# Early sub-keys of a two-layer transformer's PEER stage: weights split ahead by way of DRAM, products in three passes, and one-hot rows of eight tokens

## The chip, the cores and the metric

The kernel runs on one core of a Trainium2 chip. The metric is the device time of one execution in microseconds (us); it is measured in several runs, and their median is given. One further execution is recorded by the hardware profiler, and all the rows below are from it. The engines are named PE (TensorE, matmuls), PEld (TensorE's weight loads, which overlap PE), DVE (VectorE), ACT (ScalarE), POOL (GpSimd) and SP (SyncE, which issues most DMAs). All arithmetic is in float32 or in split products that stand for it.

## What is computed

Two layers over 512 latent tokens and 256 context tokens of width 1024. The lines of the reference that matter:

```python
u  = h * (1 + mod[:, 1]) + mod[:, 0]                  # modulate
pl = split_pieces(u @ w_mix)                          # one projection for four mixers
y  = merge_branches(u, (oa, ob, oc, od), w_gate, w_branch[l], w_out[l])
#    m = sum(sigmoid(u @ w_gate_i) * (o_i @ w_branch_i));  y = m @ w_out
h  = layer_norm(DEEPNORM_ALPHA * h + mod[:, 2] * y, ln_attn[l])
u2 = h * (1 + mod[:, 4]) + mod[:, 3]
y2 = peer_ffn(u2, peer_wq[l], peer_subkeys[l], peer_u[l], peer_v[l])
h  = layer_norm(DEEPNORM_ALPHA * h + mod[:, 5] * y2, ln_ffn[l])

def peer block(xb):                                   # 128 tokens
    s = einsum('thpk,hpnk->thpn', q, subkeys)         # 8 heads, 2 halves, 128 sub-keys
    sv, si = top_k(s, 16)
    fv, fi = top_k(all 16 x 16 sums of sv, 16)        # 16 of 16384 experts for each head
    e = first sub-key * 128 + second sub-key;  gate = softmax(fv)
    act = gelu(einsum('thkd,td->thk', tab_u[e], xb))
    return einsum('thk,thkd->td', gate * act, tab_v[e])
```

Layer 0 computes context and latent tokens; layer 1 needs only latent tokens after the mixers.

## The kernel before

**PEER, dense and sparse.** Tokens come in blocks of 128: six in layer 0, four in layer 1. For most of them (four in layer 0, three in layer 1, so `nt` is 512 or 384 columns) the expert stage is dense: for each first sub-key `j` of 128, all 128 experts are computed as a 128 x `nt` product of the table's slice `peer_ut[l, j]` (1024 x 128 floats, 512 KB) with the modulated tokens, Gelu, times a matrix `G` of gates, times `peer_v`. The other blocks gather their experts' rows by indirect DMA on POOL, beside the dense stage.

**Split products.** A float32 product that has to be exact enough is made of three matmuls of type fp32r: `split` (L107 to L110) rounds a value to its high part by an ACT copy and takes the low part by a DVE subtraction, and `mm3` (L113 to L118) multiplies high by high, high by low and low by high into the same PSUM bank. The dense stage does that for `act` (weights `du`) and `acc`, and so do the projections, the branch gates (`gate_sigmoid`, `gate_product`, weights `gw` from `wgb`) and the queries (`wq`). Products whose operands are plain float32 are issued as two matmul records each.

**The stages of a layer**, in order of the program: modulation, projections (`project_all`), `mix`, output projection, `peer_front` (layer norm, queries, the top 16 of each half), the gate stage, the dense stage, the finish. In the profiled run layer 0's mixers stand from some 240 to 560 us, its gate stage from some 1081 to 1366, and layer 1's from 2870 to 3315 and from 3484 to 3708.

**`mix`** runs the four branches in the order d, b, a, c as a generator. After each step it pays in pieces of filler: gate sigmoids (`sg`, whose result `gs` goes to DRAM as `sig`) and gate products (`pr`), by a rate for each branch (`PACE`). In layer 1 the steps also advance `mod_columns`, which makes two columns of modulation from weights that come in 512 KB loads (`wmodc`, two buffers) and are multiplied by DVE at L326. Raw q and k of each head group come back from DRAM as `src`, with `SRC` = 3 buffers.

**The gate stage** makes `G`. `chosen` (L1383 on) finds the 16 experts of each token and head, with index searches (L1404 and L1408) and predicated copies that fetch the sub-keys' numbers (L1447 to L1451), and transposes sub-keys and gates into `sT` (`pst`). `build_gates` takes `GT` = 4 tokens at a time: DVE compares a row of numbers with the tokens' sub-keys (L1474), which gives one-hot rows `ohA` and `ohB` of 4 x 128 elements, in `OHB` = 5 buffers each; ACT scales each token's `ohB` by its gates (L1480); PE multiplies the two for each token (L1484); ACT copies the product into `gs`, from where it goes to DRAM. In the third and fourth block `BD` = 1 and 2 of four tokens are compared and scaled by DVE in one instruction (L1482) in place of the long comparison and ACT.

**Early sub-keys.** So that PE has work in the gate stage, the first products of `EARLY` = 21 sub-keys in layer 0 and 26 in layer 1 are made there (`early_pieces`). For each, one 512 KB load fetches `eu` (two buffers), eight matmuls of 512 or 384 columns multiply it with `u2`, a plain float32 copy of the modulated tokens that `modulate` keeps, ACT does the Gelu, and the result goes to DRAM as `ge`. `UP` gives the share of these pieces that is due before the first one-hot row (33% and 48%), and the rest is spread over the steps of `build_gates`; in layer 0 pieces of the next layer's modulation stand among them. The dense stage then loads `ge` for these sub-keys instead of computing it.

**What sets the order.** The program is written in the Tile framework, whose scheduler places each instruction on its engine's queue by priority and readiness in a modelled time line; `tc.later(n)` lowers the priority of what stands in it, `issue_after` binds it behind an instruction. Each engine then works through its queue in order, so an instruction that waits holds all behind it. SP's queue of DMA issues is one of these.

## Time and profile before

| | us |
|---|---|
| median of 3 runs | 4694.86 |
| lowest and highest | 4692.51, 4699.5 |
| the profiled execution | 4695.4 |
| its span in the profile | 4693.6 |
| PE busy in the span | 4506.4 |
| DVE busy | 3708.0 |
| ACT busy | 2310.1 |
| POOL busy | 1004.5 |

The mean clock granted to TensorE over the span was 0.982 of full speed. The busy times are sums over the whole program, which goes through stages with different limits. For a stage one reads the stretch of time that it takes: how long each engine is busy in it, and what its waits end on. A busy PE is modelled from pipelined matmuls, so it isn't PE at its peak.

### The profile page before, as it was taken

The numbers are of one execution on the slowest core, as the hardware profiler recorded it, in microseconds if no ns is written. First come the engines' busy times: TensorE is split into PE (matmuls) and PEld (weight loads), VectorE is DVE, ScalarE is ACT, GpSimd is POOL, SyncE is SP. The second block draws the span as 40 slices with busy tenths as digits, with TensorE's granted clock in tenths as the row PEclk, the third lists the DMA queues.
The fourth block names the chain that finished last, engine by engine and source line by source line (L and its number), as shares of the span: only waits on it lengthen the run. The fifth ranks groups of instructions, "written<-read, shape, count | busy, mean of one in ns | idle before, by whom it ended". The sixth has DMA issues, their size and how long they took to land.

```text
span 4693.6 us, 67460 instructions
## 1 busy us (share of the span) xinstructions
PE 4506.4 (96%) x24113; PEld 3820.5 (81%) x24113; DVE 3708.0 (79%) x7649; ACT 2310.1 (49%) x4214; POOL 1004.5 (21%) x772
## 2 busy tenths in 40 slices
PE   8999999999999999999999798898999999999998
PEld 6978888885668888888888697787877788888887
DVE  7857555899979889898889975866698777777777
ACT  4357554325964444344334454665328744444444
POOL 0000000000005545555555200000000043333431
PEclk9999999999999999999999899999999999999999
DMA  7844332523679999999999676542426798888885
GB/s 276 293 144 125 105 99 90 206 78 115 182 246 339 347 337 348 341 346 348 343 341 345 215 280 189 176 145 87 168 89 179 246 351 309 303 310 295 313 304 196
DMA packets 495793, 1120.39 MB, mean 239 GB/s; under 512 B 43312, under 2 KB 244832, under 8 KB 486368
## 3 DMA queue, kind: packets, MB, share of 16 engines
q1 hardware_dynamic: 384864, 713.38, 44.9%
q0 software_dynamic: 110592, 402.70, 23.9%
q8 instruction: 190, 3.11, 0.3%
q14 instruction: 147, 1.20, 0.1%
HBM read 975.14 MB, written 140.80 MB: 238 GB/s over the span
## 4 chain that ended last, share of the span: by engine, by line
PE 73%; issue 8%; DVE 7%; ACT 5%; DMA 4%; POOL 2%; SPq 0%; POOLq 0%; DVEq 0%; ACTq 0%
PE act L115 5%; PE act L117 5%; PE act L116 5%; PE acc L117 5%; PE acc L115 5%; PE acc L116 5%; PE S L1506 4%; PE mm L117 3%; PE mm L115 3%; PE mm L116 3%; PE mm L1484 3%; PE sg L115 3%; PE sg L116 3%; PE sg L117 3%; PE mm L124 2%
## 5 line engine op out<-in xcount | busy, mean ns | idle before, releaser
L1678 POOL DMA_INDIRECT gu<-peer_u,pe x384 | 494.7, 1288 | 3049.5 <-DMA du<-peer_ut 2515.8
L1690 POOL DMA_INDIRECT gu<-peer_v,pe x384 | 509.6, 1327 | 569.4 <-PE acc L117 252.4
L115 PE MATMUL act<-u2T,duh 128*128 128x512 f32 (+1 forms) x1656 | 603.5, 364 | 11.8 <-ACT duh L109 11.8
L117 PE MATMUL act<-u2T,dul 128*128 128x512 f32 (+1 forms) x1656 | 603.4, 364 | 0.7 <-DVE dul L110 0.7
L116 PE MATMUL act<-u2T,duh 128*128 128x512 f32 (+1 forms) x1656 | 602.8, 364 | 0.0
L115 PE MATMUL acc<-dvh,dwh 128*128 128x512 f32 x1536 | 598.5, 390 | 2.3 <-ACT dwh L109 2.3
L116 PE MATMUL acc<-dvl,dwh 128*128 128x512 f32 x1536 | 599.4, 390 | 0.0
L1696 DVE SCALAR_TENSOR_TENSOR gy<-gu,gwt,gy 128x1024 f32<-128x1024 f32 x381 | 488.2, 1281 | 106.1 <-DMA gu<-peer_v,pe 102.5
L117 PE MATMUL acc<-dvh,dwl 128*128 128x512 f32 x1536 | 546.6, 391 | 1.8 <-DVE dwl L110 1.8
L1681 DVE SCALAR_TENSOR_TENSOR gu<-gu,px 128x1024 f32<-128x1024 f32 x384 | 462.6, 1221 | 92.7 <-DMA gu<-peer_u,pe 91.9
L109 ACT ACTIVATE dwh<-dw 128x512 fp32r<-128x512 f32 (+1 forms) x256 | 147.8, 578 | 555.9 <-DVE dw L1566 553.0
L1565 ACT ACTIVATE dw<-Gt 128x512 f32<-128x512 f32 (+1 forms) x256 | 260.3, 1020 | 278.3 <-DVE dwl L110 274.7
L109 ACT ACTIVATE dvh<-dv 128x1024 fp32r<-128x1024 f32 x256 | 263.4, 1052 | 206.9 <-PE rot L117 122.8
L115 PEld LDWEIGHTS act<-u2T,duh 128*128 128x128 f32 x1656 | 312.2, 189 | 50.3 <-ACT duh L109 12.5
L110 DVE TENSOR_TENSOR dvl<-dv,dvh 128x1024 fp32r<-128x1024 f32 x256 | 309.5, 1220 | 52.6 <-ACT dvh L109 52.5
L116 PEld LDWEIGHTS act<-u2T,duh 128*128 128x128 f32 x1656 | 312.3, 189 | 37.3
L117 PEld LDWEIGHTS act<-u2T,dul 128*128 128x128 f32 x1656 | 312.1, 188 | 37.2 <-DVE dul L110 2.3
L117 PEld LDWEIGHTS acc<-dvh,dwl 128*128 128x128 f32 x1536 | 287.8, 188 | 65.7 <-DVE dwl L110 6.2
L115 PEld LDWEIGHTS acc<-dvh,dwh 128*128 128x128 f32 x1536 | 288.3, 188 | 60.8 <-ACT dwh L109 4.0
L116 PEld LDWEIGHTS acc<-dvl,dwh 128*128 128x128 f32 x1536 | 288.3, 188 | 57.5
L1484 PEld LDWEIGHTS mm<-ohB,ohA 128*128 128x128 f32 x1792 | 234.0, 193 | 98.8 <-ACT ohB L1480 48.7
L1506 PE MATMUL S<-u,eu 128*128 128x384 f32 (+1 forms) x752 | 310.7, 537 | 2.0 <-ACT ege L1509 1.2
(396 smaller groups left out, 10873.8 us busy)
## 6 DMA issues: line engine op xcount, KB each, us to landing
dv<-peer_v SPq DMA_DIRECT2D x256, 512.0 KB, 6.1
du<-peer_ut SPq DMA_DIRECT2D x207, 512.0 KB, 6.3
G<-gsb SPq DMA_DIRECT2D x26, 2048.0 KB, 9.3
wmodc<-wmodc SPq DMA_DIRECT2D x84, 512.0 KB, 5.1
gw<-wgb SPq DMA_DIRECT2D x128, 256.0 KB, 2.9
Gt<-G SPq DMA_DIRECT2D x31, 1024.0 KB, 8.3
eu<-peer_ut SPq DMA_DIRECT2D x49, 512.0 KB, 3.8
Gt<-G SPq DMA_DIRECT2D x31, 768.0 KB, 6.7
```

Of the source, the lines that this page charges most:

```text
L109: a = self.nc.scalar.activation(hi, src, AF.Copy)
L110: return a, self.nc.vector.tensor_tensor(lo, src, hi, op=OP.subtract)
L115: mm(out, lh, rh, start=first, stop=False)
L116: mm(out, lh, rl, start=False, stop=False)
L117: self.pe = mm(out, ll, rh, start=False, stop=last)
L1484: self.last = nc.tensor.matmul(ps[:, s % 4, :], A[:, s, :], B[:, s, :], start=True, stop=True)
L1506: nc.tensor.matmul(ps[:, :n], U[:, k, :], uf[:, k, :], start=k == 0, stop=k == KC - 1)
L1565: nc.scalar.activation(W, self.Gt[:, :, j % JB], AF.Copy)
L1678: dma = nc.gpsimd.indirect_dma_start(out=t, out_offset=None, in_=I['peer_u'], in_offset=bass.IndirectOffsetOnAxis(ap=e[:, k:k + 1], axis=0))
L1681: nc.vector.scalar_tensor_tensor(t, t, 1.0, x, op0=OP.mult, op1=OP.mult, accum_out=act[:, k:k + 1])
L1690: dma = nc.gpsimd.indirect_dma_start(out=t, out_offset=None, in_=I['peer_v'], in_offset=bass.IndirectOffsetOnAxis(ap=e[:, k:k + 1], axis=0))
L1696: nc.vector.scalar_tensor_tensor(y, t, w[:, k:k + 1], y, op0=OP.mult, op1=OP.add)
```

## The change

1. **Weights split ahead.** A new generator, `split_early`, runs in `mix`. It takes the slices `peer_ut[l, j]` of the early sub-keys in parts: halves of 128 x 512 in layer 0 (42 parts), quarters of 128 x 256 in layer 1 (104). Each part is loaded into `eur` (`PREB` = 2 buffers), split by an ACT copy into `eus` (one buffer) and a DVE subtraction in place, and both halves are stored in a DRAM tile `eu`. `mix` advances it by `PRE` parts for each step of a branch: 3 in layer 0's branch d, 2 in layer 1's branches d, a and c. In layer 0 what is left is done, and its pool given back, before the sum `m` is allotted at the end of branch d; in layer 1 it shares the mixers' pool, and what is left is done at the end of `mix`.
2. **Products in three passes.** `early_pieces` loads the two halves (`euh`, `eul`, 512 KB each, two buffers each) from `eu` and calls `mm3` with the split tokens `uT` that the dense stage uses. The plain copy `u2` is gone, and `modulate` loses its argument `keep`. `first_u` has a tile of its own.
3. **Eight tokens at a time.** `GT` goes from 4 to 8, `OHB` from 5 to 3, and `BD` from 1 and 2 of four tokens to 2 and 4 of eight. L1474 (L1487 after) compares 8 x 128 elements in one instruction.
4. **`SRC`** is 3 in layer 0 and 2 in layer 1.

The diff, cut to its core:

```diff
-PKB, BIG, VB, SRC, GK = (8, 4, 4, 3, 4)
-GT, OHB = (4, 5)
+PKB, BIG, VB, SRC, GK = (8, 4, 4, (3, 2), 4)
+GT, OHB = (8, 3)
-BD = (0, 0, 1, 2)
+BD = (0, 0, 2, 4)
+PREB = 2
+PRE = ({'d': 3}, {'d': 2, 'a': 2, 'c': 2})
+PREK = (4, 2)
...
-            u = keep[:, k, c0:c0 + n] if keep is not None else pool.tile([128, 512], F, name="uf", bufs=3 if tok else 2)[:, :n]
+            u = pool.tile([128, 512], F, name="uf", bufs=3 if tok else 2)[:, :n]
...
+            self.eu = self.dram.tile([EARLY[l], 2, 128, KC, 128], F, name=f"eu{l}")
...
-                fill = [self.early_pieces(l, i, uf, tp) for i in range(EARLY[l])]
+                fill = [self.early_pieces(l, i, uT, nd * 128, tp) for i in range(EARLY[l])]
...
+            ep = tc.alloc_tile_pool(name="eus", bufs=2, side="right", reuse_waits="tile") if self.need else self.ap
...
+            pre = self.split_early(l, ep)
             at = 0
             for kind, done in self.branches(l, blocks, order):
                 at += 1
+                for _ in range(PRE[l].get(kind, 0)):
+                    next(pre, None)
...
                     if kind == 'd':
+                        if self.need:
+                            for _ in pre:
+                                pass
+                            ep.release()
                         self.dp.release()
...
+    def split_early(self, l, p):
+        nc, w = self.nc, PREK[l]
+        parts = [(i, j, slice(h, h + w)) for i, j in enumerate(early(l)) for h in range(0, KC, w)]
+        raw = []
+        for n, (i, _, ks) in enumerate(parts):
+            while len(raw) < min(n + PREB, len(parts)):
+                U = p.tile([128, w, 128], F, name="eur", bufs=PREB)
+                nc.sync.dma_start(U, self.I['peer_ut'][l, parts[len(raw)][1]][:, parts[len(raw)][2]])
+                raw.append(U)
+            hi = p.tile([128, w, 128], R, name="eus", bufs=1)
+            self.split(hi, raw[n][:].bitcast(R), raw[n])
+            for x, u in enumerate((hi[:].bitcast(F), raw[n])):
+                nc.sync.dma_start(self.eu[i, x][:, ks], u)
+            yield
...
-            U = p.tile([128, KC, 128], F, name="eu", bufs=2)
-            nc.sync.dma_start(U, self.I['peer_ut'][l, j])
+            U = [p.tile([128, KC, 128], R, name="eu" + x, bufs=2) for x in "hl"]
+            for x, u in enumerate(U):
+                nc.sync.dma_start(u[:].bitcast(F), self.eu[i, x])
             return U
...
-                nc.tensor.matmul(ps[:, :n], U[:, k, :], uf[:, k, :], start=k == 0, stop=k == KC - 1)
+                self.mm3(ps[:, :n], (U[0][:, k, :], U[1][:, k, :]), (uT[0][:, k, :n], uT[1][:, k, :n]), k == 0, k == KC - 1)
```

**Where the instructions stand.** PE, layer 0's gate stage, at its first one-hot products. `mm<-ohB,ohA` are the products of one-hot rows, one for each token; `S<-u_10140,eu` is an early product of 512 columns. Before:

```order
L1506 MATMUL S<-u_10140,eu 128x512
L1484 MATMUL mm<-ohB,ohA 128x128 x4
L1506 MATMUL S<-u_10140,eu 128x512
L1484 MATMUL mm<-ohB,ohA 128x128 x4
L1506 MATMUL S<-u_10140,eu 128x512
L1484 MATMUL mm<-ohB,ohA 128x128 x4
```

The same place now; `u2T_10432` and `u2T_10433` are the high and the low parts of the tokens, `euh` and `eul` those of the weights:

```order
L1497 MATMUL mm<-ohB,ohA 128x128 x8
L119 MATMUL S<-u2T_10432,euh 128x512
L120 MATMUL S<-u2T_10433,euh 128x512
L121 MATMUL S<-u2T_10432,eul 128x512
L119 MATMUL S<-u2T_10432,euh 128x512
L120 MATMUL S<-u2T_10433,euh 128x512
L121 MATMUL S<-u2T_10432,eul 128x512
L1497 MATMUL mm<-ohB,ohA 128x128 x8
```

One early product stood behind each four one-hot products; now one or two, of three passes each, stand behind each eight.

DVE, layer 0's gate stage, from the last instructions ahead of the first one-hot rows. `fi` and `fv` are the index searches of `chosen`, `t` and `tm` its predicated copies, `c` a copy of the candidates, `c_iota` the row of numbers. Before:

```order
L1408 MAX_INDEX fi<-fv,c_13468 128x8
L1407 MAX fv<-c_13474 128x8
L1449 COPY_PREDICATED t_12891<-tm,t_12891 128x64
L1474 TENSOR_TENSOR ohA<-c_iota,pst_10138 128x512
L1474 TENSOR_TENSOR ohB<-c_iota,pst_10138 128x512
L1474 TENSOR_TENSOR ohA<-c_iota,pst_10138 128x512
L1474 TENSOR_TENSOR ohB<-c_iota,pst_10138 128x512
```

Now:

```order
L1460 COPY_PREDICATED t_13333<-tm,sif 128x512
L1487 TENSOR_TENSOR ohA<-c_iota,pst_10437 128x1024
L1487 TENSOR_TENSOR ohB<-c_iota,pst_10437 128x1024
L1487 TENSOR_TENSOR ohA<-c_iota,pst_10437 128x1024
L1487 TENSOR_TENSOR ohB<-c_iota,pst_10437 128x1024
L1487 TENSOR_TENSOR ohA<-c_iota,pst_10437 128x1024
L1487 TENSOR_TENSOR ohB<-c_iota,pst_10437 128x1024
L1445 TENSOR_TENSOR a_13311<-fi,t_13315 128x128
L1462 COPY_PREDICATED t_13321<-tm,t_13321 128x64x4
L1419 MATCH_REPLACE c_13914<-fv,cand 128x112
L1421 MAX_INDEX fi<-fv,c_13908 128x8
L1462 COPY_PREDICATED t_13333<-tm,t_13333 128x64x4
```

The first rows stood behind the last searches and copies of the next blocks; now rows of twice the length stand ahead of a part of these.

ACT, layer 1's mixers, in branch c. `PTh`, `oT` and `OT` are copies out of PSUM for which PE waits, `P` the exponentials. Before:

```order
L882 ACTIVATE PTh<-mm 128x4x128
L882 ACTIVATE PTh<-mm 128x128
L855 ACTIVATE oT_31560<-mm 128x512
L896 ACTIVATE OT<-mm 128x256
L1004 ACTIVATE P,sums<-S,nms 128x512
L882 ACTIVATE PTh<-mm 128x4x128
L109 ACTIVATE gwh<-gw 128x256
L859 ACTIVATE oT_31561<-mm 128x512
```

Now:

```order
L895 ACTIVATE PTh<-mm 128x4x128
L895 ACTIVATE PTh<-mm 128x128
L113 ACTIVATE eus<-eur 128x256
L868 ACTIVATE oT_31546<-mm 128x512
L113 ACTIVATE eus<-eur 128x256
L909 ACTIVATE OT<-mm 128x256
L1017 ACTIVATE P,sums<-S,nms 128x512
L895 ACTIVATE PTh<-mm 128x4x128
L872 ACTIVATE oT_31547<-mm 128x512
L895 ACTIVATE PTh<-mm 128x128
L1017 ACTIVATE P,sums<-S,nms 128x640
L113 ACTIVATE eus<-eur 128x256
```

The splits of the weights (`eus<-eur`) stand between these copies, each behind its own load.

## Rows read from the trace of the kernel before

**Rows 1.** Page, part 1: busy us (share of the span) and instructions.
```profile
PE 4506.4 (96%) x24113; PEld 3820.5 (81%) x24113; DVE 3708.0 (79%) x7649; ACT 2310.1 (49%) x4214; POOL 1004.5 (21%) x772
```

**Rows 2.** Windows: us, then busy us (instructions) per engine, clock, DMA share, GB/s.
```profile
165.00:240.00 75.00, 75.00 (x627) 74.98 (x627) 65.72 (x130) 25.71 (x46) 0.00 (x0) 1.00 0.76 253
240.00:400.00 160.00, 146.38 (x824) 121.90 (x823) 96.95 (x220) 98.82 (x208) 0.00 (x0) 0.96 0.45 136
2870.00:3080.00 210.00, 190.12 (x906) 148.98 (x907) 150.61 (x311) 134.46 (x274) 0.00 (x0) 0.95 0.53 161
3080.00:3315.00 235.00, 220.41 (x1256) 185.99 (x1255) 151.71 (x297) 136.79 (x295) 0.00 (x0) 0.99 0.37 114
1081.00:1130.00 49.00, 44.19 (x106) 19.35 (x105) 49.00 (x302) 14.97 (x24) 0.00 (x0) 0.99 0.47 156
1130.00:1262.00 132.00, 122.28 (x660) 88.09 (x661) 127.62 (x398) 127.88 (x361) 0.00 (x0) 0.97 0.56 164
1262.00:1366.00 104.00, 103.57 (x601) 74.26 (x601) 90.44 (x241) 83.86 (x219) 0.00 (x0) 1.00 0.67 193
3484.00:3536.00 52.00, 50.77 (x160) 29.84 (x159) 51.72 (x297) 16.80 (x33) 0.00 (x0) 1.00 0.44 134
3545.00:3650.00 105.00, 102.14 (x612) 81.06 (x611) 83.08 (x168) 102.96 (x304) 0.00 (x0) 1.00 0.67 199
```

The engines stand in the order PE, PEld, DVE, ACT, POOL.

**Rows 3.** Time line of PE, early products: start us, us, instruction, records.
```profile
1080.92 32.78 PE L1506 MATMUL S<-u,eu 128*128 128x512 f32 x76
...
3483.40 36.29 PE L1506 MATMUL S<-u,eu 128*128 128x384 f32 x112
...
3702.46 5.33 PE L1506 MATMUL S<-u,eu 128*128 128x384 f32 x16
```

**Rows 4.** Windows, as in rows 2: 200 us of layer 0's dense stage.
```profile
1400.00:1600.00 200.00, 200.00 (x884) 165.59 (x883) 180.03 (x297) 83.26 (x98) 103.55 (x80) 1.00 0.92 341
```

**Rows 5.** Groups of DVE instructions, whole span: busy us, mean ns, idle before.
```profile
L1404 DVE FIND_INDEX8 fi<-fv,cand 128x8 uint32<-128x112 f32 x80 | 20.3, 266 | 0.0
...
L1449 DVE COPY_PREDICATED t<-tm,t 128x128 f32<-128x128 uint32 x40 | 16.8, 425 | 0.1
```

**Rows 6.** Window of tile eu alone: us, PE, PEld, DVE, ACT, clock, DMA, GB/s.
```profile
1262.00:1366.00 104.00, 49.50 (x98) 15.19 (x98) 0.00 (x0) 0.00 (x0) 1.00 0.67 193
```

**Rows 7.** DMA issues at 3470:3540, 2870:3315 and 220:560: KB each, us to landing.
```profile
eu<-peer_ut SPq DMA_DIRECT2D x10, 512.0 KB, 3.6
...
gw<-wgb SPq DMA_DIRECT2D x27, 128.0 KB, 2.4
...
qkv0ckv<-qkr SPq DMA_DIRECT2D x3, 128.0 KB, 1.8
```

**Rows 8.** Groups as in rows 5: a comparison of 512 and an operation of 1024.
```profile
L1474 DVE TENSOR_TENSOR ohA<-c_iota,pst 128x512 f32<-128x512 f32 x224 | 154.3, 689 | 12.7 <-PE mm L1484 12.3
...
L1274 DVE TENSOR_TENSOR aff<-aff,lnt 128x1024 f32<-128x1024 f32 x10 | 12.1, 1214 | 5.5 <-DMA aff<-hnorm 5.2 <-issue 0.3
```

**Rows 9.** Groups at 2870:3315: splits of the branch gates' weights.
```profile
L109 ACT ACTIVATE gwh<-gw 128x512 fp32r<-128x512 f32 x62 | 39.1, 631 | 70.4 <-PE sg L116 60.3 <-issue 8.7 <-ACT P L1004 0.6
L109 ACT ACTIVATE gwh<-gw 128x256 fp32r<-128x256 f32 x30 | 12.6, 423 | 13.0 <-PE pr L116 11.6 <-ACT pkH L808 0.8 <-ACT gs L1220 0.3
L110 DVE TENSOR_TENSOR gwh<-gw,gwh 128x256 fp32r<-128x256 f32 x30 | 12.5, 417 | 1.2 <-ACT gwh L109 1.2
```

**Rows 10.** Time line of SP: one issue of a DMA; start us, us.
```profile
3260.95 0.33 SPq L1223 DMA_DIRECT2D sig<-gs  x1
```

**Rows 11.** Tile wmodc at 2790:3320: its DVE reader, and what that waited for.
```profile
L326 DVE SCALAR_TENSOR_TENSOR mjunk<-wmodc,csrow x31: 1170/1219/1227, 2791.5 to 3088.6; 128x1024 bf16<-128x1024 f32 x31
...
  DMA wmodc<-wmodc: 18.5, 11
```

**Rows 12.** Windows, as in rows 2, in layer 1's mixers.
```profile
2960.00:3040.00 80.00, 69.50 (x348) 54.65 (x347) 68.96 (x148) 53.52 (x118) 0.00 (x0) 0.91 0.57 178
3040.00:3120.00 80.00, 78.90 (x419) 66.86 (x418) 52.20 (x96) 48.97 (x100) 0.00 (x0) 1.00 0.49 150
```

More of the change, by code (lines that the diff above doesn't have):

```diff
@@ L359, in folded, with modulate @@
         return f[:, 0], f[:, 1]
-    def modulate(self, cols, blocks, h_src, uT, tok=None, pool=None, c0=0, keep=None, ks=range(KC)):
+    def modulate(self, cols, blocks, h_src, uT, tok=None, pool=None, c0=0, ks=range(KC)):
         nc = self.nc
@@ L443, in layer @@
                 slots = [tp.tile([128, 4, 128], F, name=f"pst{i}", bufs=1) for i in range(2)]
-                uf = tp.tile([128, KC, nd * 128], F, name="u2", bufs=1)
-                top = self.peer_front(l, blocks, dense, sparse, uT, uf, kp, tp, hp)
+                top = self.peer_front(l, blocks, sparse, uT, kp, tp, hp)
                 self.ge = self.dram.tile([EARLY[l], 128, nd * 128], F, name=f"ge{l}")
@@ L652, in mix @@
             sa = ExitStack()
-            self.srcp = tc.alloc_tile_pool(name="src", bufs=SRC, side="right", reuse_waits="tile")
+            self.srcp = tc.alloc_tile_pool(name="src", bufs=SRC[l], side="right", reuse_waits="tile")
             self.ap = self.pool(sa, "att", 2)
@@ L694, in mix @@
                         (product if prods else sigmoid)()
-            for _ in cols:
-                pass
+            for x in (cols, pre):
+                for _ in x:
+                    pass
             sa.close()
@@ L795, in packed @@
         nc, p = self.nc, self.ap
-        src = self.srcp.tile([128, NB, 128], F, name="src", bufs=SRC)
+        src = self.srcp.tile([128, NB, 128], F, name="src", bufs=SRC[l])
         nc.sync.dma_start(src[:, :nb], self.dup[l, grp][:nb, :, h, :].rearrange("b p c -> p b c"))
@@ L1315, in outproj, with peer_front @@
             pass
-    def peer_front(self, l, blocks, dense, sparse, uT, uf, kp, tp, hp):
+    def peer_front(self, l, blocks, sparse, uT, kp, tp, hp):
         nc, I = self.nc, self.I
@@ L1342, in peer_front @@
                     u, c0 = (uC, 0) if b == LB else (uT, 128 * b)
-                    self.modulate(cols, blocks[b:b + w], self.z, u, self.x2, tmp, c0, uf if b < len(dense) else None)
+                    self.modulate(cols, blocks[b:b + w], self.z, u, self.x2, tmp, c0)
             hp.release()
@@ L1516, in first_u @@
         p = self.u0p = self.tc.alloc_tile_pool(name="u0", bufs=1, side="right", reuse_waits="tile")
-        U = tp.tile([128, KC, 128], F, name="eu", bufs=2)
+        U = tp.tile([128, KC, 128], F, name="fu", bufs=1)
         self.nc.sync.dma_start(U, self.I['peer_ut'][l, 0])
```

4 lines of the change are left out of this document (1 added, 3 removed).

## The prediction, as it was written before the result

> **What bounds the kernel now.** I read the page first: TensorE (PE) is busy 96% of the span [rows 1], so any PE time taken away could count. An average says nothing on a stage, though, so next I cut the two stages that the change touches out of the span [rows 2]. What the reader is to see there: in the mixers (240 to 400 us in layer 0, 2870 to 3315 us in layer 1) PE is the fullest engine, idle 13.6 us and 19.9 + 14.6 = 34.5 us, and ScalarE (ACT) is busy only 62% and 61%. In the gate stage, where DVE makes one-hot rows, ACT scales them, PE multiplies them and the early products fill PE's gaps, all three are nearly full at once. Layer 0's first two blocks (1130 to 1262) have ACT at 127.9 and DVE at 127.6 of 132 us, PE at 122.3; its last two (1262 to 1366) have PE at 103.6 of 104, DVE at 90.4, ACT at 83.9. Layer 1's first two blocks (3545 to 3650) have ACT at 103.0 of 105. So a shorter PE instruction is paid back in full in only one of these rows.
>
> **The early products.** 38 products of 512 columns follow each other in 32.78 us, 0.862 us each; 56 of 384 columns in 36.29 us, 0.648 us [rows 3]. The new form is three passes of the kind that fill the dense stage: 884 of 512 columns in 200 us, 0.226 us each [rows 4], so 0.678 us for three; scaled by columns, three of 384 take 0.510 us (an estimate from that row). Saved: 168 products x 0.184 = 31 us in layer 0, 208 x 0.138 = 29 us in layer 1, 60 us of PE in all. What comes through, stage by stage:
> - Layer 0 before the first gate product (1081 to 1130): DVE is busy 49 of 49 us [rows 2], so PE's gain is worth nothing there. But in the new order DVE reaches its first one-hot row with some eight index searches (0.266 us) and six predicated copies (0.425 us) of later blocks still behind it [rows 5]: 2.1 + 2.6, about 4 us earlier, of which one more long multiply takes some back, and they come due later beside other work. I take -4.
> - Layer 0, blocks 0 and 1: ACT runs the same scalings as before; it has 4.1 us of idle to give. I take -2.
> - Layer 0, blocks 2 and 3: PE is the bound. 98 records, 49 products, stand in that stretch [rows 6]: 49 x 0.184 = 9. DVE, next with 13.6 us to spare, and ACT, with 20, let it through. -9.
> - Layer 1, ahead of the gates (3484 to 3536): before, 64 products stood before the first transpose (41.5 us); now 218 passes (37 us by the row). But a sub-key's piece now needs two 512 KB loads where it had one, and one lands in 3.6 us [rows 7]. Two beside each other land in 3.6 to 7.2 us; with two buffers and 4.1 us of passes a piece lasts at best 4.1 and at worst (7.5 + 4.1) / 2 = 5.8 us, 37 to 53 us for 9.1 pieces. Between them, +3; DVE is full there (51.7 of 52) and hides some: +2, with ends -4 and +11.
> - Layer 1, blocks 0 and 1: ACT's idle is 2.0 us; -2.
> - Layer 1, end: before, eight products stand behind the last gate product, 16 records in 5.33 us [rows 3]; now six passes, 1.0 us. -4.
> Sum: -15 in layer 0, -4 in layer 1, **-19 us of the 60**. Ends: -8 (only the end of layer 1 and half of the rest) and -46 (everything in the stretches where PE is over 97% busy, with the idle of the others).
>
> **One-hot rows of eight tokens.** A row of 512 elements costs DVE 0.689 us, an op of 1024 elements 1.214 us [rows 8], so each pair of rows saves 0.16 us: 64 pairs of A in layer 0 and 48 in layer 1 give 18 us, the shorter B rows at most as much again. This is DVE time in stretches where ACT or PE ends last; I price it at nothing by itself. Without it DVE (127.6 of 132) would hold what PE gives in layer 0, so it is part of the -19. The scalings by ACT stay the same in number: four in eight tokens go to DVE in the last block as two in four did. With three buffers of eight tokens instead of five of four DVE may run 24 tokens ahead instead of 20, so no new wait arises there.
>
> **The weights that are split ahead.** 42 parts of 512 columns in layer 0 and 104 of 256 in layer 1; each is a load, an ACT copy, a DVE subtraction and two stores. ACT takes 0.631 or 0.423 us, DVE 0.417 for the small ones [rows 9]. 14 of layer 0's stand while the projections still run: there PE is 75.0 of 75 and ACT 25.7 [rows 2], so that work is hidden, but 14 x 0.79 MB on top of 253 GB/s brings the queue near 380 GB/s, and at the end of the projections the mixers' first loads wait for stores: +3. The other 28 are 18 us on ACT's 98.8. I let PE's idle grow as ACT's load does: 13.6 x 18% = +2. In layer 1, 104 x 0.423 = 44 us on 271, 16% of 34.5 us: +6. **Sum +11.**
> What may hide or undo that is the round trip. A buffer of raw weights (two) waits for copy, subtraction, store, and next load; by the rows 0.42 + 0.42 + 1.8 + 2.4 us and two issues of 0.33 us, 5.7 us for two parts, 2.9 us a part [rows 7, 9, 10]. The new order puts layer 1's copies, counted against the `gs` instructions that stand beside them in the trace, 3.3 to 4.6 us apart nearly everywhere, so the data should mostly be there. Where it isn't, ACT stands still in its own queue, and behind it stand the `PTh`, `OT` and `P` copies for which PE waits. SP too gets 485 more issues, of which the stores wait for ACT and DVE; behind them stand `gw` and `src` loads. `SRC` of 2 in layer 1 shortens that lead. Bounds of the whole group: 0 (all of it in ACT's idle 38%) and +65 (below).
>
> **Sum.** The profiled run took 4695.4 us (span 4693.6), beside a median of 4694.9, so both give the same sum: 4695.4 - 19 + 11 = **4687 us**, 0.17% less. A difference of about 0.2%, 9.4 us, is what a measurement of this kernel can tell from none; this forecast lies just inside, with much of its own range outside.
>
> **Rivals.**
> *Splits that stall the mixers.* The nearest row is the stream of modulation columns, loaded two ahead in the same way: DVE waited 18.5 us before 11 of 31 of them, and PE was idle 10.5 of 80 us in the stretch that has most of them, against 1.1 in the next [rows 11, 12], about 0.9 us for each of ten. If every split costs a quarter of that, 0.25 us x 146 = +37 in place of +11: 4713 us. At 0.45 us each it is +65, 4741. For it: ACT's in-order queue, and a stretch with 13 splits in a row where the order leaves 2.3 us each, under the round trip. Against: those loads were four times as large, and DVE was at 86% there. It turns the sign at (19 + 9.4) / 146 = 0.19 us of PE for each split.
> The Trainium skill, "DMA: Bandwidth & Descriptors", in the part on where the two microseconds go, says that a DMA's fixed cost is about 2.0 us however small it is, and advises large transfers; by its fit a 128 KB DMA takes 2.3 us, and the round trip would be 3.0 us a part. That speaks against these small stores, and the rows (1.8 and 2.4 us) agree on the size.
> *The gate stage isn't PE's at all.* In blocks 2 and 3 PE's weight loads are busy only 74.3 of 104 us [rows 2]; if PE's 103.6 is an appearance of pipelined records, the bound is the chain DVE, ACT, PE of each token group, and the -9 and half of the other terms are lost: -8 + 11, 4698 us.
> "Perfetto Trace Analysis" in the Trainium skill, under identifying the most-contended engine, says this of matmul busy time, that it is a poor measure and weight-load occupancy a better one. By that rule the time would be this rival's; the 32.78 us of products with no gap speak for PE being really occupied.
> *PE alone decides.* If all of the 46 us comes through and the splits fit into idle time: 4649 us.
>
> **How the numbers follow.** Forecast 0.40 (its own range 4676 to 4698: faster 0.18, same 0.21, slower 0.01). Stalls 0.26 (slower 0.23, same 0.03). Not PE's 0.16 (same 0.14, slower 0.02). PE alone 0.18, faster. Faster 0.36, same 0.38, slower 0.26. The range goes from PE alone, 4649, to between the two prices of stalls, 4728; what is beyond on either side is about 2 in 10.
>
> **What would show it.** Products: `S` records of about 0.39 us in threes, with starts 0.23 us apart. Gate stage: from the first one-hot row to the first `act` product 15 us less in layer 0, about 5 less in layer 1, and ACT, not PE, above 95% in both. Mixers: PE idle 5 us more in layer 0 and 6 in layer 1, and waits of ACT's `eus` on the `eur` loads below 20 us in sum. It is wrong if those waits reach 50 us and PE's idle there grows by 30 (stalls), or if blocks 2 and 3 don't shorten although PE is no longer full (not PE's).

## The result, and the profile after

The changed kernel takes **4823.0 us** (median of 4 runs, 4817.9 to 4828.7), beside 4693.7 us for the kernel before on the same chip: a ratio of 1.0275, 95% interval 1.026 to 1.029. I had forecast 4687 with a range up to 4728. It is 129 us slower; the rival of the stalled mixers had been given 4713 us, 18 slower.

The page of the changed kernel, parts 1 and 2 (first line: the busy us, shares and instructions that [rows 1] has of before; second: the granted clock of PE in 40 slices of the span):

```profile
PE 4524.7 (94%) x24489; PEld 3928.2 (81%) x24489; DVE 3757.1 (78%) x7571; ACT 2362.3 (49%) x4358; POOL 1012.8 (21%) x772
...
PEclk9989999999999999999999898899999999999999
```

PE is busy 18 us longer although early products got shorter, and its share of the span has fallen. To find the place I took the same instructions of both traces as marks: the last branch product of layer 0's mixers (`pr`), the last product of the sub-key scores, with which the gate stage is taken to begin, the first product of the dense stage (`act`), and so on. In layer 1 the mixers' first mark is a transposition of modulation columns into a tile `sg`; it stands 37 us before the end of the projections in both kernels. By these marks layer 0's mixers reach to 825 us, not to some 560 as the section on the kernel before has it: branch c and the branch products go on after that.

| stretch | before, us | after, us | difference |
|---|---|---|---|
| start to the last branch product of layer 0 | 825.5 | 860.8 | +35.3 |
| output projection and queries, layer 0 | 255.6 | 257.9 | +2.3 |
| gate stage, layer 0 | 288.5 | 280.5 | -8.0 |
| dense stage, layer 0, and on to layer 1's first mark | 1450.9 | 1450.0 | -0.9 |
| layer 1's mixers (first mark to last branch product) | 488.8 | 590.3 | +101.5 |
| output projection and queries, layer 1 | 174.3 | 171.4 | -2.9 |
| gate stage, layer 1 | 223.7 | 219.8 | -3.9 |
| dense stage, layer 1 | 972.8 | 979.4 | +6.6 |

The last line isn't the change's: over the other profiles of this study that stage took 968 to 984 us, and before's profile is at the short end. What is left is plain: **+137 us in the mixers of both layers, -12 us in the gate stages.** Layer 0's 35 us all stand ahead of its first branch product, which moved from 377.8 to 412.7 us; from there to the last one it takes 447.5 us before and 447.8 after. In the stretch ahead of it, from 242 us on, the granted clock was 0.89 instead of 0.96 and the DMA share 0.78 instead of 0.44.

Windows of the two mixers before (columns as in [rows 2]: us, then busy us and instructions of PE, PEld, DVE, ACT and POOL, granted clock, DMA share, GB/s):

```profile
240.00:825.50 585.50, 557.55 (x3413) 484.21 (x3412) 342.50 (x703) 331.84 (x765) 0.00 (x0) 0.98 0.36 111
2820.50:3309.30 488.80, 448.35 (x2450) 370.80 (x2447) 317.98 (x643) 281.73 (x591) 0.00 (x0) 0.97 0.48 148
```

and after:

```profile
240.00:860.80 620.80, 573.41 (x3415) 491.60 (x3414) 364.17 (x742) 346.48 (x797) 0.00 (x0) 0.96 0.46 148
2849.20:3439.50 590.30, 484.98 (x2450) 394.33 (x2449) 356.92 (x747) 316.11 (x695) 0.00 (x0) 0.90 0.61 192
```

In layer 1, ACT and DVE have the 104 instructions more that the splits bring, 34 and 39 us of work. PE has the same 2450 records, yet the stretch is 101.5 us longer: PE is idle 105.3 us instead of 40.5, which is 64.9 us, and its unchanged work takes 36.6 us more at a granted clock of 0.90 instead of 0.97. (448.35 x 0.97 = 435 and 484.98 x 0.90 = 436: the whole of the second part is the clock.)

What ACT and DVE waited for, by form, after, 2849 to 3440 us (busy us, mean ns, idle just before, and what ended it):

```profile
L113 ACT ACTIVATE eus<-eur 128x256 fp32r<-128x256 f32 x104 | 43.4, 417 | 134.7 <-DMA eur<-peer_ut 73.2 <-DMA eu<-eus 49.9 <-issue 3.1
L114 DVE TENSOR_TENSOR eur<-eur,eus 128x256 fp32r<-128x256 f32 x104 | 43.8, 422 | 95.4 <-ACT eus L113 95.2
```

And SP's queue of DMA issues in the same stretch (total us, times, longest):

```profile
SPq L1513 <- DMA eu<-eur: 102.1, 71, 4.0
SPq L1519 <- ACT eus L113: 57.0, 46, 3.4
```

ACT stood 123 us before its 104 copies: 73 for the load, 50 for the store of the part before, which still held the one `eus` buffer. DVE stood 95 us for ACT, and SP 102 us before the next load, because the store of the low half still held one of the two `eur` buffers. Each is an in-order queue, and everything behind stands too. Ten microseconds of it, after, on ACT, DVE, SP and PE (start us, us, instruction, and in brackets the idle time before it and what ended that; SP's list has no brackets):

```profile
2998.34 0.42 ACT L113 ACTIVATE eus<-eur 128x256 fp32r<-128x256 f32 x1 [1.45 <-DMA eu<-eus]
...
3000.70 0.63 ACT L113 ACTIVATE PTh<-SD 128x512 fp32r<-128x512 f32 x1 [0.45 <-DVE SD L1194]
3005.31 0.42 ACT L113 ACTIVATE eus<-eur 128x256 fp32r<-128x256 f32 x1 [3.97 <-DMA eur<-peer_ut]
3005.63 0.61 ACT L113 ACTIVATE PTh<-SD 128x512 fp32r<-128x512 f32 x1
...
3005.76 0.43 DVE L114 TENSOR_TENSOR eur<-eur,eus 128x256 fp32r<-128x256 f32 x1 [3.70 <-ACT eus L113]
...
3000.48 0.33 SPq L1513 DMA_DIRECT2D eur<-peer_ut  x1
...
3001.40 0.39 SPq L1217 DMA_DIRECT2D gw<-wgb  x1
3004.93 0.33 SPq L1513 DMA_DIRECT2D eur<-peer_ut  x1
3005.32 0.43 SPq L810 DMA_DIRECT2D src<-dup1bk  x1
...
2998.26 0.39 PE L1175 MATMUL S<-PTl,VV 128*128 128x512 f32 x1
2998.49 0.39 PE L1175 MATMUL S<-PTh,VV 128*128 128x512 f32 x1
...
3002.11 0.50 PE L1175 MATMUL S<-PTl,VV 128*128 128x512 f32 x1
3006.30 0.50 PE L1175 MATMUL S<-PTh,VV 128*128 128x512 f32 x1 [3.69 <-ACT PTh L113]
...
3009.15 0.63 PE L121 MATMUL sg<-u,gwh 128*128 128x512 f32 x1
3009.58 0.63 PE L119 MATMUL sg<-u,gwh 128*128 128x512 f32 x1
```

The load issued at 3000.48 isn't there when ACT comes to its split at 3001.34; it takes some 4.8 us, from its issue to ACT's start, twice the 2.4 us that loads of this size took before [rows 7]. ACT stands 3.97 us; DVE, behind it, 3.70; the `PTh` that PE needs stands behind the split on ACT, and PE idles 3.69 us for it. SP, too, does nothing from 3001.8 to 3004.93, and a `src` load stands behind the `eur` load. Then PE's products follow each other 0.43 us apart, where they stood 0.23 apart at 2998: the lower of the clock's two levels, 1.2 instead of 2.4 GHz, after the idle time. For most of the time that PE stands neither ACT nor DVE works; the DMA engines do (a share of 0.68 from 3000 to 3010).

### The profile page after: what moved, and what is told of

Same layout as the page of the kernel before. It is cut to its first block, busy times and chain, and to the rows that moved or that the text cites. A ratio compares the mean times of both kernels' runs of the same rounds, so it can differ in the third digit from the quotient of the medians.

```text
span 4823.8 us, 69236 instructions
## 1 busy us (share of the span) xinstructions
PE 4524.7 (94%) x24489; PEld 3928.2 (81%) x24489; DVE 3757.1 (78%) x7571; ACT 2362.3 (49%) x4358; POOL 1012.8 (21%) x772
## 5 line engine op out<-in xcount | busy, mean ns | idle before, releaser
L1707 POOL DMA_INDIRECT gu<-peer_u,pe x384 | 509.8, 1327 | 3163.8 <-DVE fi L1421 1425.7
L121 PEld LDWEIGHTS acc<-dvh,dwl 128*128 128x128 f32 x1536 | 288.3, 188 | 64.2 <-DVE dwl L114 3.8
L113 ACT ACTIVATE duh<-du 128x1024 fp32r<-128x1024 f32 x207 | 218.5, 1056 | 186.3 <-PE act L120 182.1
L119 PE MATMUL sg<-u,gwh 128*128 128x512 f32 (+1 forms) x768 | 287.5, 374 | 16.0 <-ACT gs L1233 14.1
```

The costliest lines, as they stand in the source:

```text
L113: a = self.nc.scalar.activation(hi, src, AF.Copy)
L119: mm(out, lh, rh, start=first, stop=False)
L121: self.pe = mm(out, ll, rh, start=False, stop=last)
L1707: dma = nc.gpsimd.indirect_dma_start(out=t, out_offset=None, in_=I['peer_u'], in_offset=bass.IndirectOffsetOnAxis(ap=e[:, k:k + 1], axis=0))
```

## The experiments

All times are medians; the difference is to the kernel before on the same chip. The two stretches in the middle are of each kernel's trace: the start to layer 0's last branch product (825.5 before) and layer 1's mixers (488.8 before).

| kernel | us | difference | layer 0 to its last branch product | layer 1's mixers |
|---|---|---|---|---|
| split_only | 4839.8 | +142 | 857.9 | 591.5 |
| no_store | 4761.2 | +63 | 841.9 | 531.4 |
| no_load | 4773.2 | +79 | 841.0 | 546.1 |
| work_only | 4734.8 | +37 | 841.7 | 511.1 |
| work_two | 4731.2 | +37 | 841.9 | 507.7 |
| work_dve | 4722.5 | +28 | 843.6 | 498.6 |
| work_act | 4700.4 | +5 | 822.0 | 498.9 |
| src2 | 4697.6 | +3 | 824.0 | 488.7 |
| two_eus | 4810.2 | +116 | 859.5 | 570.3 |
| deep_l1 | 4812.3 | +115 | 886.4 | 554.2 |
| dma_pool | 4836.7 | +141 | 871.3 | 537.7 |
| dma_pool_two | 4820.6 | +126 | 870.9 | 539.4 |
| sub_pool | 4815.9 | +122 | 865.2 | 577.6 |
| pool_split | 4826.6 | +132 | 915.4 | 504.0 |
| gt4 | 4826.3 | +128 | 858.2 | 591.3 |
| oh8 | 4715.3 | +18 | 825.2 | 491.5 |
| one_split | 4690.7 | -7 | 822.8 | 494.7 |
| pool_gate | 4777.4 | +80 | 824.5 | 486.9 |

**Is it the splits at all?** *split_only* is the kernel before with `split_early` and `SRC` of the changed one; `early_pieces`, `u2`, `GT`, `OHB` and `BD` are those before.

> The kernel before with the splits in the mixers and SRC of 2 in layer 1; what they store is not read, and the early products are the plain ones, four tokens at a time. Theory A (the splits in the mixers are the whole loss, since the later stages of the changed kernel got shorter by some 7 us): mixers longer by about 35 us in layer 0 and 100 us in layer 1, gate stages as before, 4815 to 4840 us. Theory B (the loss needs the new products or the long one-hot rows as well): under 4770 us.

4839.8 us, ratio 1.030 (1.0285 to 1.032). Both mixers are as long as in the changed kernel, the gate stages as before (288.3 and 223.8). Theory A holds: the splits are the whole loss and more.

*src2* is the fourth, silent part of the change by itself:

```diff
-PKB, BIG, VB, SRC, GK = (8, 4, 4, 3, 4)
+PKB, BIG, VB, SRC, GK = (8, 4, 4, (3, 2), 4)
```

> The kernel before with SRC of 2 instead of 3 in layer 1, nothing else. Theory: the 22 us that work_only loses in layer 1's mixers are the 104 copies and subtractions, so this one is within 5 us of before, 4692 to 4702 us. If the missing src buffer is behind them: 4708 to 4720 us.

Ratio 1.0002 (0.9992 to 1.0013), layer 1's mixers 488.7: no part in it.

**What of a split costs?** Three kernels take pieces out of *split_only*. In *work_only* a resident part is split again and again:

```diff
+        raw = p.tile([128, w, 128], F, name="eur", bufs=1)
+        nc.sync.dma_start(raw, self.I['peer_ut'][l, parts[0][1]][:, parts[0][2]])
         for n, (i, _, ks) in enumerate(parts):
-            while len(raw) < min(n + PREB, len(parts)):
-                U = p.tile([128, w, 128], F, name="eur", bufs=PREB)
-                nc.sync.dma_start(U, self.I['peer_ut'][l, parts[len(raw)][1]][:, parts[len(raw)][2]])
-                raw.append(U)
             hi = p.tile([128, w, 128], R, name="eus", bufs=1)
-            self.split(hi, raw[n][:].bitcast(R), raw[n])
-            for x, u in enumerate((hi[:].bitcast(F), raw[n])):
-                nc.sync.dma_start(self.eu[i, x][:, ks], u)
+            lo = p.tile([128, w, 128], R, name="eul", bufs=1)
+            self.split(hi, lo, raw)
```

> As split_only, but each split reads one resident part and writes two tiles that nothing reads: the same 146 ACT copies and 146 DVE subtractions at the same places of the program, 2 loads, no stores. Theory A1 (ACT, DVE and SP stand still for loads and stores of a part, round after round): hardly any of the loss is left, 4700 to 4715 us. Theory A2 (the added work of ACT and DVE is the loss): over 4790 us.

*no_store* keeps the loads and the split as they are and has no stores:

> As split_only with all its loads, but nothing is stored. If the one buffer of high parts, which the next copy gets only when its store has landed, is the larger wait: 4715 to 4750 us. If the loads that come two ahead are the larger wait: over 4780 us.

*no_load* is *work_only* with the stores of `hi` and `lo`:

> As work_only (4735 us), with both stores of every part, from one buffer each for high and low parts. If the stores' round trip is the larger part of the loss, as the 78 us between no_store and split_only say: 4790 to 4830 us. If stores hurt only together with loads, whose buffers they hold: under 4765 us.

4734.8, 4761.2 and 4773.2 us, none of them in a range that I had given. The work alone costs 37 us, between my two theories; loads alone add 27, stores alone 38, and both together 105, more than their sum of 65. They hold each other up: a load can't start before the store has freed its buffer, and a store's round trip then has a load's behind it. By layers: in layer 0 the work takes 16 of the 35 us, loads alone or stores alone add nothing to it, and only both together make the rest; in layer 1 the work takes 22 of the 101, loads alone add 20, stores alone 35. In *no_store*, where no store holds a copy, the wait for loads is 46 us in layer 1 (tile `eus`, 2700 to 3600 us; idle us, times):

```profile
  DMA eur<-peer_ut: 46.0, 41
  ACT eus L113: 40.2, 40
```

**Which of the work?** *work_act* does the copies of *work_only* without the subtractions, *work_dve* the subtractions without the copies (from one resident `hi`), and *work_two* is *work_only* with a second `eus` buffer in layer 1.

> As work_only (4735 us, 37 us over before: 16 in layer 0's mixers, 22 in layer 1's), with the 146 copies on ACT alone and no subtractions. If ACT's copies stand in the way of what PE waits for: 4720 to 4735 us. If it is DVE's subtractions: 4697 to 4712 us.

> As work_only (37 us over before), with the 146 subtractions alone on a resident pair of tiles, so that no DVE instruction waits for a copy; work_act, with the copies alone, lost 4 us. If DVE's time is what work_only loses: 4720 to 4735 us. If it is the wait of each engine's queue for the other, copy after subtraction and subtraction after copy: 4697 to 4712 us.

> As work_only, with a second high buffer in layer 1, so that a copy doesn't wait for the subtraction of the part before it. If the waits of the queues for each other are what work_only loses: layer 1's mixers from 511 to under 503 us, 4720 to 4728 us in all. If it is DVE's time: 508 to 514 us there, 4730 to 4738 us.

In total the copies alone cost nothing that can be told (1.0009, 0.9999 to 1.0018), the subtractions 28 us (1.0053, 1.0036 to 1.0069). The difference lies in layer 0, where the subtractions cost 18 us and the copies none; in layer 1's mixers each costs 10, where *one_split*, with four splits, is 6 longer than before. The scheduler put work that waits for nothing closer together than the changed kernel's splits are: *work_dve*'s subtractions in the two layers (count, ns, first and last start):

```profile
L1517 DVE TENSOR_TENSOR eul<-eur,eus x104: 372/418/428, 2897.2 to 3005.6; 128x256 fp32r<-128x256 f32 x104
...
L1517 DVE TENSOR_TENSOR eul<-eur,eus x42: 643/684/693, 153.1 to 252.9; 128x512 fp32r<-128x512 f32 x42
```

So these are prices of the work in an order of its own. Still, in layer 0 DVE's side of the splits, which my prediction left at nothing, is the dear one. The second buffer in *work_two* takes 3 us off layer 1's mixers and nothing that shows in the total: that engines wait for each other within a split is a small part.

**Buffers.** *two_eus* is the changed kernel with one more buffer, in layer 1 alone; *deep_l1* has four raw and three high ones there, in space taken from the `pk` tiles.

The edit of *two_eus*, and below it what *deep_l1* has in the place of its first new line, and besides:

```diff
-        raw = []
+        raw, PB, EB = [], (PREB, 2)[l], (1, 2)[l]
...
-            while len(raw) < min(n + PREB, len(parts)):
-                U = p.tile([128, w, 128], F, name="eur", bufs=PREB)
+            while len(raw) < min(n + PB, len(parts)):
+                U = p.tile([128, w, 128], F, name="eur", bufs=PB)
...
-            hi = p.tile([128, w, 128], R, name="eus", bufs=1)
+            hi = p.tile([128, w, 128], R, name="eus", bufs=EB)
```

```diff
-PKB, BIG, VB, SRC, GK = (8, 4, 4, (3, 2), 4)
+PKB, BIG, VB, SRC, GK = (7, 4, 4, (3, 2), 4)
...
+        raw, PB, EB = [], (PREB, 4)[l], (1, 3)[l]
```

> The changed kernel with two buffers instead of one for the high parts (eus) in layer 1; layer 0 untouched. Theory A1 (a copy on ACT waits until the store of the one before it has landed, and all behind it on ACT, then DVE, SP and PE): layer 1's mixers, 590 us, get 30 to 60 us shorter, 4765 to 4795 us, and the waits of ACT's eus on the DMA eu<-eus, 50 us in layer 1, all but vanish. Theory A3 (SP's queue and the traffic of DMAs are the wait, whatever the buffers): within 10 us of 4823.

> The changed kernel with four raw buffers and three high ones in layer 1, paid for with 7 instead of 8 pk buffers in both layers. Layer 1's mixers took 590 us in the changed kernel, 570 with a second high buffer, 511 with the work alone. Theory A1 (round trips): with these buffers most waits on eur and eus are gone and they take 515 to 545 us, 4745 to 4780 us in all. If the traffic itself is what is left: 560 us or more, over 4790 us.

Layer 1's mixers go from 590 to 570 and 554 us, so the direction is A1's, and the size falls short of what I expected of either, in the totals too. In *two_eus* the wait for the store is gone as expected, but most of it has become a wait for the load (tile `eus`, 2700 to 3600 us):

```profile
  DMA eur<-peer_ut: 92.7, 52
  ACT eus L113: 85.0, 53
  issue: 19.2, 11
```

In *deep_l1* the waits for loads and stores are 57 and 12 us. It loses in layer 0 what it gains in layer 1: with 7 `pk` buffers the mixers there take 886 instead of 861 us, so its total says nothing on the splits.

**Which queue?** *dma_pool* issues the loads and stores of the splits on POOL's queue; *dma_pool_two* adds the second `eus` buffer in layer 1; *sub_pool* leaves the DMAs on SP and does the subtractions on POOL, with that buffer; *pool_split* does all four steps on POOL.

The edit of *sub_pool* (*pool_split* has `nc.gpsimd.tensor_copy(hi, raw[n])` as its first new line), and below it that of the three others on the DMAs:

```diff
-            self.split(hi, raw[n][:].bitcast(R), raw[n])
+            nc.scalar.activation(hi, raw[n], AF.Copy)
+            nc.gpsimd.tensor_tensor(raw[n][:].bitcast(R), raw[n], hi, op=OP.subtract)
```

```diff
-                nc.sync.dma_start(U, self.I['peer_ut'][l, parts[len(raw)][1]][:, parts[len(raw)][2]])
+                nc.gpsimd.dma_start(U, self.I['peer_ut'][l, parts[len(raw)][1]][:, parts[len(raw)][2]])
...
-                nc.sync.dma_start(self.eu[i, x][:, ks], u)
+                nc.gpsimd.dma_start(self.eu[i, x][:, ks], u)
```

> The changed kernel with copy, subtraction, loads and stores of the splits on POOL and its own DMA queue, which are idle in the mixers. Theory A1: ACT, DVE and SP no longer wait, so the mixers are near those before and the 12 us of the gate stages are left: 4680 to 4720 us; layer 0's first branch products still wait for the last split, which at some 6 us a part on POOL comes at about 390 us. Theory A3 (DMA traffic in the mixers is the loss): over 4780 us.

> The changed kernel with loads and stores of the splits issued on POOL's queue instead of SP's; copies stay on ACT, subtractions on DVE, buffers as they were. If SP's queue, which stood 102 us before loads into eur and so held the loads of the mixers behind it, carries the stall: layer 1's mixers get from 590 to under 550 us, 4750 to 4790 us in all. If ACT's own queue carries it (copies that wait for a landing hold the copies for which PE waits): 575 us or more there, 4805 to 4835 us.

> As dma_pool, with two buffers for the high parts in layer 1. In dma_pool layer 1's mixers had got from 590 to 538 us, but the last split came 38 us behind their end, and PE stood for the weights of the output projection, whose space the splits' buffers held. If that reading holds, a quicker chain of parts ends inside the mixers: 520 to 545 us for them and the usual 172 behind instead of 225, 4770 to 4790 us in all. If SP has no part in it and the 538 are paid back in another way: over 4815 us.

> The changed kernel with the subtractions on POOL (copies on ACT, DMAs on SP) and two high buffers in layer 1. If DVE's queue, in which a subtraction stands until ACT's copy is done (95 us in layer 1 of the changed kernel), carries the stall: layer 1's mixers 500 to 535 us (two_eus: 570), layer 0's 10 to 20 us shorter, 4735 to 4780 us. If ACT's queue carries it: within 10 us of two_eus, 4800 to 4820 us.

None is much faster than the changed kernel in all, and the totals alone would mislead: *pool_split*'s stands where I had put the traffic of DMAs, *dma_pool_two*'s where SP has no part, *sub_pool*'s where it is ACT's queue, and *dma_pool*'s just above its ranges. The stretches tell more. With everything on POOL, layer 1's mixers take 504 us, with 89 of the 104 splits inside them: the traffic, 207 GB/s there, and POOL's own interference cost some 15 of the 101 us. With only the DMAs moved off SP they take 538 and 539 us, so about half of the loss in layer 1 goes with SP's queue. With only the subtractions moved off DVE they take 578, no better than *two_eus* with 570. That speaks against DVE's long waits behind ACT as what PE waited for, but doesn't rule them out, as a subtraction takes POOL 0.74 us there (median) and DVE 0.42. The other half holds the work and ACT's waits for these DMAs, 78 us in *dma_pool* and 68 in *dma_pool_two*; how it divides isn't shown.

The gain is paid back behind the mixers. In *dma_pool* POOL's chain of parts ends 38 us after the last branch product, the tiles still hold space that the weights of the output projection are to have, and PE stands for them (waits, 3380 to 3460 us: total us, times, longest):

```profile
PEld mm L119 <- ACT wh L113: 45.3, 3, 40.9
PE mm L119 <- ACT wh L113: 44.4, 3, 40.4
```

In *dma_pool_two* the last split starts 4 us after the mixers' end instead of 38, and of the 52 us paid behind them 32 are still paid, where I had expected none: the late splits explain less than half. In *pool_split* 37 us come behind layer 1's mixers, and layer 0's end 90 us late although its first branch product comes 13 us late; I traced that no further than that its last split starts at 440.8 us, and that the sum `m` is allotted only after the splits' pool is given back.

**The gains by themselves.** *gt4* is the changed kernel with one-hot rows of four tokens, *oh8* the kernel before with rows of eight (three `ohA`, two `ohB` buffers). *one_split* is the changed kernel with `enumerate(early(l)[:1])` in `split_early` and `self.eu[0, x]` in `early_pieces`; it leaves out 140 of the 146 splits.

> The changed kernel with one-hot rows of four tokens as before. My prediction priced long rows at nothing by themselves: 4820 to 4835 us, and the gate stages 0 to 10 us longer than with eight. If the long rows cost something: under 4815 us.

> The kernel before with one-hot rows of eight tokens alone (three ohA and two ohB buffers, for space). Prediction: nothing by itself, 4690 to 4700 us; if DVE's 18 us come through where DVE is full: 4680 to 4688 us; if scalings by ACT in trains of eight make PE wait: over 4702 us.

> The changed kernel, but only the first early sub-key's weights are split in the mixers (2 parts in layer 0, 4 in layer 1), and every early piece loads that one pair from DRAM; so the products of the other early sub-keys are made with the wrong weights, and 140 of the 146 splits are left out. Theory: the mixers are as before and the 12 us of the gate stages come through to the end: 4679 to 4688 us. If something later pays them back: within 5 us of before.

*gt4* differs from the changed kernel by 3 us, and its gate stages take 279.8 and 219.1 us beside 280.5 and 219.8: beside products in three passes the long rows are worth nothing, as forecast; but the forecast that without them DVE would hold what PE gives didn't come true either. *oh8* costs 18 us (1.004, 1.0026 to 1.0053), as the rival of ACT's trains has it; its profile has 2 and 6 us of that in the gate stages and the rest spread in pieces of 3 us and less, besides the layer 1 dense stage that varies anyway. In layer 0's gate stage it doesn't bear that rival out: PE's weight loads wait 31.6 us for ACT's `ohB`, 43.2 before. DVE, though, waits 11.6 us for PE before its `ohB` rows, as it didn't before. Whether the third `ohB` buffer that it lacks is the cause of the 18 us isn't settled. *one_split* gains 7 us (0.9984, 0.9975 to 0.9993); its gate stages take 279.7 and 220.3 us, 12 us less than before. So the products' gain is real and small, a little smaller than I expected of this kernel.

**Splitting where the weights are used.** *pool_gate* has no splits in the mixers and no trip through DRAM: POOL, idle in the gate stages, splits each early sub-key's weights as it is loaded there. Rows of four tokens, `SRC` of 3.

```diff
+            raw = p.tile([128, KC, 128], F, name="eur", bufs=1)
+            nc.sync.dma_start(raw, self.I['peer_ut'][l, early(l)[i]])
             U = [p.tile([128, KC, 128], R, name="eu" + x, bufs=2) for x in "hl"]
-            for x, u in enumerate(U):
-                nc.sync.dma_start(u[:].bitcast(F), self.eu[i, x])
+            nc.gpsimd.tensor_copy(U[0], raw)
+            nc.gpsimd.tensor_tensor(U[1], raw, U[0], op=OP.subtract)
```

> Products in three passes, one-hot rows of four tokens, no splits in the mixers and no trip through DRAM: each early sub-key's weights are loaded once in the gate stage and split there by POOL, which is idle in it, into the tiles that PE reads; SRC is 3. Theory A1 (the loss stands in the mixers only): mixers as before, gate stages 12 us shorter as in the changed kernel, 4680 to 4688 us. Rival: POOL slows the subtractions and comparisons of DVE while it works (688 ns became 833 in pool_split), 80 us of POOL in layer 0's gate stage and 100 in layer 1's at 20 to 40% are 15 to 35 us of DVE, which bounds half of these stages: 4690 to 4710 us.

The mixers are as before, 824.5 and 486.9 us: without splits there, no loss there. The gate stages take 323.7 and 268.0 us, 35 and 44 more: the rival, and beyond its range. Three windows of layer 0's gate stage, to set beside [rows 2]:

```profile
1081.00:1130.00 49.00, 29.95 (x124) 23.57 (x123) 49.00 (x270) 13.60 (x20) 14.12 (x8) 0.79 0.30 102
1130.00:1262.00 132.00, 108.97 (x644) 94.79 (x643) 128.97 (x344) 108.12 (x303) 45.07 (x18) 0.94 0.51 152
1262.00:1366.00 104.00, 86.06 (x546) 75.61 (x546) 103.80 (x250) 81.24 (x215) 26.11 (x12) 0.97 0.56 167
```

and DVE's comparisons in the whole of that gate stage, 1081 to 1404 us, by form (x count, busy us, mean ns):

```profile
L1481 DVE TENSOR_TENSOR ohA<-c_iota,pst 128x512 f32<-128x512 f32 x128 | 92.8, 725 | 3.0 <-PE mm L1491 3.0
L1481 DVE TENSOR_TENSOR ohB<-c_iota,pst 128x512 f32<-128x512 f32 x64 | 60.9, 951 | 0.0
```

DVE is now full nearly from end to end, 103.8 of 104 us even where PE was, and a comparison of 512 that takes 0.689 us alone [rows 8] takes up to 0.951 on average beside POOL. The Trainium skill, "Perfetto Trace Analysis", under optimizing scalar and DVE operations, warns of this: the two engines share a read port of SBUF, so that moving work from one to the other might not help. The rows agree that it didn't help; they show the slower comparisons, not the port.

No version that makes all the products rightly beat the kernel before: the gate stages' 12 us are all that there is to win, and the cheapest place found for the splits costs more.

## Why the prediction was wrong

**The bound, and the products.** These steps held in the main. By PE's marks, in layer 0 the time to the first gate product fell by 0.7 us (forecast 4), the first two blocks by 0 (2), the last two with the end by 7 (9): -8 for -15. In layer 1: +2.6 ahead of the gates (+2), -4.3 in the first two blocks (-2), +1.5 in the third (0), -3.8 at the end (-4): **-4 for -4**, with some luck, as two errors of about 2 us cancel. Together -12 where I said -19, inside my bounds of -8 and -46. "PE alone decides" fell; and that blocks 2 and 3 of layer 0 got shorter speaks against "isn't PE's at all", though the sum of -12 is nearer to that rival's -8 than to mine. In these blocks the sign "ACT, not PE, above 95%" did not come: PE is still busy 97.7 of 100 us, ACT 82.7 (columns as above):

```profile
1299.00:1399.00 100.00, 97.69 (x655) 83.46 (x654) 85.14 (x180) 82.67 (x220) 0.00 (x0) 1.00 0.76 226
```

Of the earlier start of DVE's one-hot rows nothing came through: DVE stayed full (48.7 of 48.7 us) to the first product.

**The splits.** Here it failed, by +137 for +11, and the step can be named: "5.7 us for two parts, 2.9 us a part". From it followed that "the data should mostly be there" and that PE's idle would grow only as ACT's load does, +2 and +6 of the +11. I had divided a part's round trip by the two raw buffers. But the high half has one buffer, `eus`, and a copy into it waits until the store before it has landed; and SP, in whose queue loads and stores stand between those of the mixers, doesn't issue them at once. In layer 1 the copies came from 2901.5 to 3362.5 us, 461 / 104 = **4.4 us a part**, in layer 0 from 152.1 to 419.9, 6.4 us. ACT stood idle before most of them, 135 of the 461 us in all; without that they would come 3.1 us apart (an estimate, 326 / 104), so the room of 3.3 to 4.6 us between copies, on which I relied, wasn't there either. Of the two omissions SP's queue weighs more: a second `eus` buffer gave layer 1's mixers back 20 of the 101 us (*two_eus*), the DMAs off SP's queue 53 (*dma_pool*), though these were paid back behind them. The price of one transfer was nearly right in layer 1: in *two_eus* the loads landed in 2.4 us and the stores in 2.5 and 2.9 (medians), for my 2.4 and 1.8. By the fit in the Trainium skill, "DMA: Bandwidth & Descriptors", in the part on where the two microseconds go, which I cited, and which the page gives for DMAs issued by GpSimd, a DMA of 128 KB takes about 2.3 us, an estimate; these, issued by SP, agree on the size. Layer 0's parts of 256 KB, for which I had no price, landed in 3.9 to 4.3 us there. What was wrong in the main was how many wait for each other.

I did draw the rival that came true, and named its row: the modulation columns, "about 0.9 us for each of ten" waited-for loads. Then I took a quarter of that, because those loads were four times as large and DVE fuller. Measured: 137 us / 146 splits = **0.94 us for each**, the undiscounted row. That the two figures are the same is partly luck: the row counts idle PE for each waited-for load, while the 0.94 also holds the work of the splits (37 us in *work_only*) and the lost clock (36.6 us in layer 1). In the row's own unit, layer 1 has 64.9 us more of idle PE for 72 waits of ACT's copies, 0.90 at most. The turning point of 0.19 us was passed fivefold.

**DVE.** Of 11 us, eight were for ACT's load, three for the DMA queue at the end of layer 0's projections, and none for DVE's. With the copies alone the kernel lost 5 us, with the subtractions alone 28. In layer 0 I counted 14 splits as hidden behind full PE from 165 to 240 us, and looked at ACT, 25.7 of 75 us; DVE, in the same row [rows 2], was at 65.7 of 75, and 14 more of 0.69 us are 9.7, more than its 9.3 of idle. Ten came before 240 us, and the rest in branch d. (The same 14 would also have brought the queue to 253 + 147 = 400 GB/s over these 75 us, not to near 380.)

**The clock.** No term of the sum had it. Of layer 1's 101.5 us, 36.6 are the same PE records at a lower granted clock, so each microsecond more of idle PE went with 1.6 us of time there.

**Signs named in advance.** "Waits of `eus` on `eur` below 20 us in sum" would show it right, "50 us, and PE's idle grown by 30" the stalls: in layer 1 alone they were 73 us, and the idle grew by 65. That sign decided for the stalls.

What stays open: how the second half of layer 1's loss divides between ACT's waits and the work itself in its true places, why in layer 0 loads and stores cost only together, why layer 0's mixers end late in *pool_split*, and why *oh8* is slow.

## What to carry to other kernels

Work that goes through DRAM and back in a stage of dependent steps is priced by its period, the round trips of all its buffers with the waits of the queue that issues them, not by its busy time; where the order gives it less room than that period, each piece stops the in-order queues that it stands in, here ACT's and SP's. Take the nearest row of a waited-for load at its full price, and count the idle time of PE with what the clock takes on top. And of a split, cost every engine that it uses in the stretch where it will stand, not only the one with the name.

## What the runs showed of the hardware

- After a PE gap of 3.7 us, products of 512 columns stood 0.43 us apart, at the level of 1.2 GHz, and later 0.23 us again; over layer 1's mixers, with 65 us more of idle PE, the granted clock was 0.90 instead of 0.97 (the changed kernel).
- Beside POOL's copies and subtractions, DVE's subtractions of 512 elements on the gates' weights (`gwh`) took 833 ns on average instead of 688 (*pool_split*), and its comparisons up to 951 instead of 689 (*pool_gate*).
- A copy of 128x256 took POOL 0.40 us, as long as ACT's 0.42, and the subtraction 0.75, beside DVE's 0.42; issuing one DMA took POOL 0.54 to 0.56 us and SP 0.33 to 0.38 (medians, *pool_split* and the changed kernel).
